# An attention stage whose softmax scaling moves behind the output product, in a lane of its own

## The chip, the cores and the metric

The kernel runs on one core of a Trainium2 chip. Five engines work from queues of their own: the matrix engine (PE in the profile, its weight loads shown apart as PEld), VectorE (DVE), ScalarE (ACT), GpSimd (POOL) and SyncE (SP), which here only issues transfers. SBUF is the working memory, PSUM the eight banks into which PE writes, DRAM the large memory outside. The metric is device time in microseconds (us) from the first to the last instruction of the program; smaller is better.

## The reference

Two layers over 1024 tokens of width 1024. Layer 0 mixes with a recurrence, layer 1 with attention; each layer then has a squared-ReLU MLP and a gated embedding. The change lies in the attention of layer 1, and in what stands around it:

```python
def chunk_band_attention(h, w_qkv, q_g, k_g, rel_bias):
    qkv = (h @ w_qkv).reshape(bsz, seq, 3, C_HEADS, C_HEAD_DIM)      # 16 heads x 64
    q = rmsnorm(qkv[:, :, 0], q_g) * (C_HEAD_DIM ** -0.5)
    k = rmsnorm(qkv[:, :, 1], k_g)
    v = qkv[:, :, 2]
    ...
        s = jnp.einsum('bqhd,bkhd->bhqk', q_c, k_b).astype(jnp.float32) + bias
        s = jnp.where(valid, s, -jnp.inf)
        prob = jax.nn.softmax(s, -1).astype(v.dtype)
        return jnp.einsum('bhqk,bkhd->bqhd', prob, v_b)              # own chunk of 64 and 8 before it
```

`h` is the RMS-normalised residual stream: each token's row is divided by the root of its mean square and multiplied by a learned gain. The result of the attention goes through `attn_w_out` and is added to the stream.

## The kernel before, in words

**Products.** Every value that enters a matmul is split into two parts (hi and lo, type float32r), and a product is three matmuls (hi with hi, hi with lo, lo with hi). ACT copies the hi part, DVE subtracts to get lo.

**Steps.** The attention runs over 16 steps `s = (pr, hf)`: `pr` is one of 8 pairs of heads, `hf` one of the two halves of the tokens (512 each). A step has three parts.

- `attn_in` projects: for each of 4 tiles of 128 tokens (`e`, tile number `i`) 24 matmuls of 128x384 give q, k and v of the pair in one PSUM bank. The gain is in `xg` already; the division by the root mean square is done after the product, as ACT copies q and k (`qk`) and v (`vs`) out of the bank with the factor `rscol[:, i]`. DVE subtracts for v's lo part. `rscol` is made once, in `row_stats`, right after the first projection: 16 small matmuls against ones sum POOL's squares (`accs`) over the width, and a chain of small DVE instructions takes the inverse root. Then POOL squares q and k, and DVE applies the head norm. At `hf == 0` the pair's weights (`load_qkv`, three loads of 512 KB) and bias tables (`toep`, two loads, three buffers) are loaded on SP's queue.
- `attn_norm` transposes q and k on PE into a dense bank, and ACT and DVE split them.
- `attn_block` is called for each of 2 heads `h` and 2 blocks `blk` of 256 queries. For each 128 queries `m` PE makes the scores against near keys (`sn`, bias added on DVE with a running maximum) and far keys (`sf`); ACT takes the exponential into `pb` and the sum over the row into `l`; DVE takes the reciprocal of the sum and ACT scales `pb` by it (L1973, L1974). After a pause `pb` is transposed on PE (`pt`), split (`ptile`, L349 and L350), and multiplied with v into `po`. At the second block the head's output is added up into `y` (128 rows: two heads of 64; 512 tokens), and after the second head `y` is stored to DRAM (`yd`, L2022).

**Who runs when.** `run` executes lanes (generators) in a simulated time: each lane traces instructions up to its next `yield`, and that yields a pause from the table `LAT` (in us), or a mark to wait for, such as `("at", s)`: step `s` finished. Of the lanes that are due, the first in the list goes on. There are two lanes of `attn_lane`, which share the blocks, then `attn_norms`, then `attn_ins`, which is at most three steps ahead of the finished ones. This order of tracing is the priority with which the compiler then orders each engine's queue; instructions of one engine run in that order.

**After the last step of projections** the lane `attn_ins` goes on with the gated embedding's projection (`ple_proj`) and the first half of the output projection (`out_early`), which reads `yd` back; four keys (marks) say what each of its parts waits for.

**PSUM.** Two banks (`dense`) serve projections and the transposes of the norms; in the attention two are for `sn`, one for `sf`, two for `pt`, one for `po`.

Of the kernel before, what the change touches and what calls it, by code (L numbers as in the profile page):

```python
# [8 lines left out]
F32 = mybir.dt.float32  # L9
# [8 lines left out]
P = 128  # L18
# [65 lines left out]
    "gdn_back4": 1.83,  # L84
    "attn_norm0": 0.24,
    "attn_block0": 0.97,
    "attn_block1": 4.45,
    "attn_block2": 0.43,
    "attn_block3": 0.94,
    "qk": 11.25,  # L90
    "norm": 1.28,
    "end_front": 46.33,
# [17 lines left out]
class Trunk:  # L110
# [252 lines left out]
            nc.scalar.activation(sq, src, AF.Square)  # L363
            nc.gpsimd.tensor_tensor(acc, acc, sq, op=ALU.add)

    def row_stats(self, accs, out, scale=1.0 / D, eps=1e-6):

        nc = self.nc
        nt = out.shape[-1]
        ps = self.stat_bank()  # L370
        for i in range(nt):
            self.mm(ps[:, i:i + 1], accs[i // 4][:, (i % 4) * P:(i % 4 + 1) * P], self.ones[:, 0:1],
                             start=True, stop=True)
        ms = self.sm.tile([P, NT], F32, tag="ms", name="ms")[:, 0:nt]
        nc.vector.tensor_scalar(ms, ps[:, 0:nt], scale, eps, op0=ALU.mult, op1=ALU.add)
        self.rsqrt_small(out, ms, [P, nt], "n")
# [1361 lines left out]
    def layer1_in(self):  # L1738
        nc, tc, a = self.nc, self.tc, self.a
        with ExitStack() as es:  # L1740
            self.psm = es.enter_context(self.pool("psml1", space=PSUM))
            wp = self.wp = es.enter_context(self.pool("l1a", 2))
            self.wr = es.enter_context(self.pool("l1wr", 2))
            self.w1 = es.enter_context(self.pool("l1w1"))
            l1 = es.enter_context(self.pool("l1", 2))
            self.sm = es.enter_context(self.pool("sml1", 2))
            self.yd = [[self.dr.tile([P, HB], F32, tag=f"yd{k}{hf}", name="yd") for hf in range(2)] for k in range(NK)]
            rbl = l1.tile([P, 16], F32, tag="rbl", name="rbl", bufs=1)
            nc.sync.dma_start(out=rbl, in_=a["rb_last"].rearrange("(o c) -> o c", o=1).broadcast_to((P, 16)))

            steps = [(pr, hf) for pr in range(8) for hf in range(2)]
            self.st = {}

            self.ql = [[pool.tile([P, HB], F32R, tag=tag, name="Ql", bufs=1) for pool, tag in
                        ((self.accp, f"acc{e}"), (l1, f"Ql{e}"))] for e in range(2)]
            jobs = iter([(s, h, b) for s in range(16) for h in range(2) for b in range(2)])
            self.run([self.attn_lane(steps, jobs, l1, rbl) for _ in range(2)] + [self.attn_norms(steps, l1), self.attn_ins(steps, l1)])

    def attn_ins(self, steps, l1):
        kv = {}  # L1760
        for s, (pr, hf) in enumerate(steps):
            if s >= 3:
                yield ("at", s - 3)
            self.st[s] = yield from self.attn_in(pr, hf, l1, kv)
            self.mark(("qk", s), self.lat["qk"])

        act = self.act
        ws = {}

        def load_w(src):  # L1770
            n = ws["n"] = ws.get("n", -1) + 1
            if n % 3 == 0:
                ws["h"], ws["l"] = self.weights3(n // 3 % 2)
            raw = self.wr.tile([P, T], F32, tag="wraw", name="wraw")
            self.nc.sync.dma_start(out=raw, in_=src)
            hi, lo = ws["h"][:, n % 3, :], ws["l"][:, n % 3, :]
            self.nc.scalar.copy(hi, raw)
            self.nc.vector.tensor_tensor(lo, raw, hi.bitcast(F32), op=ALU.subtract)
            return hi, lo
        p = [act([P, 2, T], F32R, "b") for _ in range(2)]  # L1780
        acc = act([P, 2, HB], F32)
        t = [act([P, 2, 2, HB], F32) for _ in range(4)]
        yield from self.ple_proj(1, lambda k, hf: p[k][:, :, hf * HB:hf * HB + HB], acc, lambda n: t[n // 2][:, n % 2],
                                 lambda: self.wp.tile([P, HB], F32, tag="sq", name="sq", bufs=1), load_w)
        q = {}

        def xt():
            n = q["n"] = q.get("n", -1) + 1
            if n % 4 == 0:
                q["x"] = act([P, 4, HB], F32)  # L1790
            return q["x"][:, n % 4, :]
        yield from self.out_early(1, self.xd, lambda q: act([P, 2, 2, HB], F32R), xt, load_w,
                                  [("at", 14), ("at", 14), ("at", 14), ("at", 15)])

    def attn_norms(self, steps, l1):
        K = []
# [10 lines left out]
    def attn_lane(self, steps, jobs, l1, rbl):  # L1807

        for s, h, b in jobs:
            yield ("in", s)  # L1810
            yield from self.attn_block(s, *steps[s], h, b, l1, rbl)

    def weights3(self, odd):

# [13 lines left out]
    def attn_in(self, pr, hf, l1, kv):  # L1828
# [15 lines left out]
        qk = wp.tile([P, 4, 256], F32, tag="qk", name="qk")  # L1844
        vs = l1.tile([P, 4, 2, P], F32R, tag="vs", name="vs", bufs=4)
        kv["vs"] = kv["vs"] + [vs]
        for e in range(4):
            i = 4 * hf + e
            ps = self.bank([P, 3, P])
            ts = slice(i * P, i * P + P)  # L1850
            for k in range(NK):
                ks = slice(k * P, k * P + P)
                xh, xl = self.xg[k][:, 0, ts], self.xg[k][:, 1, ts]
                self.mm(ps, xh, wh[:, :, ks], start=k == 0, stop=False)
                self.mm(ps, xh, wl[:, :, ks], start=False, stop=False)
                self.mm(ps, xl, wh[:, :, ks], start=False, stop=k == NK - 1)
                yield 0
            if pr == 0 and i == 0:
                self.row_stats(self.accs, self.rscol)
            rc = self.rscol[:, i:i + 1]  # L1860
            A.activation(qk[:, e, :], ps[:, 0:2, :].rearrange("p a c -> p (a c)"), AF.Copy, scale=rc)
            v3 = ps[:, 2, :].rearrange("p (h d) -> p h d", h=2)
            vf = vs[:, e].rearrange("p h c -> p (h c)").rearrange("p (q d) -> p q d", d=64)
            hi = vf[:, 0:4:3, :]
            A.activation(hi, v3, AF.Copy, scale=rc)
            V.scalar_tensor_tensor(vf[:, 1:3, :], v3, rc, hi.bitcast(F32), op0=ALU.mult, op1=ALU.subtract)  # L1866
            yield 0
        q4 = qk.rearrange("p i c -> p (i c)").rearrange("p (n d) -> p n d", d=64)
        ss = self.sm.tile([P, 16], F32, tag="ss1", name="ss1")
# [37 lines left out]
    def attn_block(self, s, pr, hf, h, blk, l1, rbl):  # L1907
# [36 lines left out]
        for j, (b, o, c0, c1) in place.items():  # L1944
            used[b] = max(used[b], o + c1 - c0)
        probs = []
        for m in (m0, m0 + 1):
            n0 = max(0, m - 2)
            nn = m - n0 + 1
            f0 = max(0, m - 4)  # L1950
            nf = n0 - f0
            pn = psm.tile([P, HB], F32, tag="sn", name="sn", bufs=2)
            score(pn[:, 0:nn * P], m, n0, nn)
            mx = sm.tile([P, 4], F32, tag="mx", name="mx", bufs=4)
            pb = self.wp.tile([P, 5 * P], F32, tag="pb", name="pb", bufs=4)
            S = pb[:, nf * P:(nf + nn) * P]
            V.tensor_tensor_reduce(S, pn[:, 0:nn * P], toep[:, (3 - nn) * P:], op0=ALU.add, op1=ALU.max,  # L1957
                                   scale=1.0, scalar=NEG, accum_out=mx[:, 0:1])
            l = sm.tile([P, 4], F32, tag="l", name="l", bufs=4)
            if nf:  # L1960
                pf = psm.tile([P, HB], F32, tag="sf", name="sf")
                score(pf[:, 0:nf * P], m, f0, nf)
                if m >= 4:
                    V.memset(pf[64:128, 0:64], NEG)
                V.reduce_max(mx[:, 1:2], pf[:, 0:nf * P], axis=AX.X)
                V.tensor_scalar(mx[:, 2:3], mx[:, 0:1], mx[:, 1:2], -1.0, op0=ALU.max, op1=ALU.mult)
                A.activation(pb[:, 0:nf * P], pf[:, 0:nf * P], AF.Exp, bias=mx[:, 2:3], accum_out=l[:, 1:2])
            else:
                V.tensor_scalar(mx[:, 2:3], mx[:, 0:1], -1.0, None, op0=ALU.mult)
            A.activation(S, S, AF.Exp, bias=mx[:, 2:3], accum_out=l[:, 0:1])  # L1970
            if nf:
                V.tensor_tensor(l[:, 0:1], l[:, 0:1], l[:, 1:2], op=ALU.add)
            V.reciprocal(l[:, 2:3], l[:, 0:1])  # L1973
            A.activation(pb[:, 0:(nf + nn) * P], pb[:, 0:(nf + nn) * P], AF.Copy, scale=l[:, 2:3])  # L1974
            probs.append((pb, f0))
            yield "attn_block0"
        yield "attn_block1"
# [30 lines left out]
                q += 1  # L2008
        if blk == 1:
            if h == 0:  # L2010
                st["y"] = l1.tile([P, HB], F32, tag="y", name="y", bufs=1)
            y, po = st["y"], st["po", h]
            oth = slice(64 * (1 - h), 64 * (1 - h) + 64)
            tmp = l1.tile([P, HB], F32, tag="otmp", name="otmp", bufs=1)
# [2 lines left out]
            if h == 1:  # L2017
                if s == 15:
                    yield ("ylast", 0)
                    self.split_scaled(self.ylast, y, None, slice(0, HB))  # L2020
                else:
                    nc.sync.dma_start(out=self.yd[pr][hf], in_=y)  # L2022
                self.dump("y1", y, (pr, slice(None), slice(hf * HB, hf * HB + HB)))
                self.mark(("at", s))
# [92 lines left out]
```

## Time and profile before

| | us |
|---|---|
| median of 3 runs | 3092.8 |
| lowest and highest | 3088.66, 3096.78 |
| the profiled execution | 3089.73 |
| its span, first to last instruction | 3088.0 |

The profiled execution's granted clock of PE is 0.978 of full speed on average. In time from the start of the span, layer 0 takes the first part, the projections of the attention begin at 1681, the first scores come at 1734, step 13 is finished at 2232 and step 15 at 2310; the rest is the output projection, the MLP and the gated embedding of layer 1.

A line of the profile such as `dps<-wq,act` names what an instruction writes and reads. `[4.11 <-POOL acc L1627]` says that the engine was idle for 4.11 us before it and that POOL's instruction of line 1627 ended that. Busy time of PE is modelled from pipelined matmuls; a stretch in which PE is busy throughout is not one in which it does its most.

### The profile page before, as it was taken

The page shows a single profiled execution, that of the slowest core. Times are in us where ns is not written, and L with a number is a line of the kernel's source. Part 1 is how long each engine was busy: PE and PEld are TensorE (multiplying, and loading weights), DVE is VectorE, ACT ScalarE, POOL GpSimd, SP SyncE. Part 2 cuts the span into 40 slices and gives each one's busy share as a digit, 9 for nine tenths or more (in the row PEclk, how much of TensorE's full clock was granted, in tenths as well). Part 3 has the DMA queues.
Part 4 walks back from the last instruction along what each step waited for, and adds up shares of the span by engine and source line. Part 5 has one row for each costly group of instructions (what it writes and reads, how often), then busy time and mean ns, then how long its engine had stood idle before and what let it go on. Part 6 is the DMA issues. An engine that isn't in the chain of part 4 may idle for free.

```text
span 3088.0 us, 47130 instructions
## 1 busy us (share of the span) xinstructions
PE 2979.5 (96%) x17288; PEld 2461.2 (80%) x17288; DVE 2232.1 (72%) x4518; ACT 1510.7 (49%) x2922; POOL 544.9 (18%) x978
## 2 busy tenths in 40 slices
PE   7999999999999999999999999989899999999999
PEld 5777778777777888888887988888788888888887
DVE  6656676657849788878867666766768888888762
ACT  4333443334427544444434577777756544544431
POOL 6533442443500000000015111100110000000002
PEclk9999999999999999999999999999999999999999
DMA  4211112211346434754424101100256444754432
GB/s 138 72 54 62 55 55 74 62 53 64 125 158 219 158 148 150 259 167 150 137 89 144 34 33 36 53 33 16 72 177 225 151 154 150 255 172 150 126 109 102
DMA packets 187639, 358.45 MB, mean 116 GB/s; under 512 B 45712, under 2 KB 47888, under 8 KB 187408
## 3 DMA queue, kind: packets, MB, share of 16 engines
q1 hardware_dynamic: 158608, 303.00, 29.6%
q10 hardware_dynamic: 28800, 52.44, 4.4%
q8 instruction: 136, 2.23, 0.3%
q14 instruction: 95, 0.78, 0.1%
HBM read 262.04 MB, written 93.32 MB: 115 GB/s over the span
## 4 chain that ended last, share of the span: by engine, by line
PE 79%; DVE 10%; ACT 4%; DMA 3%; POOL 2%; issue 2%; SPq 0%; DVEq 0%; POOLq 0%; ACTq 0%
PE dps L177 66%; PE ch L177 2%; PE pm L177 2%; PE iz L177 1%; PE po L177 1%; PE tp L177 1%; DVE ptile L350 1%; PE pt L192 1%; DVE pb L1957 1%; PE sn L177 1%; POOL subt L415 1%; PE py L177 1%; DMA wraw<-in_w_qkv 1%; ACT pb L1970 1%; POOL sub L417 1%
## 5 line engine op out<-in xcount | busy, mean ns | idle before, releaser
L177 PE MATMUL dps<-r,act 128*128 128x512 f32 x3528 | 829.4, 392 | 0.0
L177 PEld LDWEIGHTS dps<-r,act 128*128 128x128 f32 x3528 | 662.0, 188 | 145.8
L177 PE MATMUL dps<-xg,whi 128*128 128x512 f32 x1280 | 434.0, 419 | 14.9 <-ACT xg L352 7.4
L1614 POOL TENSOR_TENSOR pn<-pn,prs 128x512 f32<-128x512 f32 x32 | 47.1, 1474 | 1543.1 <-ACT prs L386 1447.7
L177 PE MATMUL dps<-wq,act 128*128 128x384 f32 x1536 | 305.7, 345 | 6.4 <-DVE vs L1866 3.1
L177 PEld LDWEIGHTS dps<-xg,whi 128*128 128x128 f32 x1280 | 233.9, 195 | 67.9 <-issue 8.0
L177 PEld LDWEIGHTS dps<-wq,act 128*128 128x128 f32 x1536 | 266.6, 191 | 10.5 <-DVE vs L1866 4.9
L177 PE MATMUL dps<-xg,wlo 128*128 128x512 f32 x640 | 258.8, 405 | 1.3 <-DVE wlo L304 1.3
L177 PE MATMUL dps<-late,act 128*128 128x512 f32 x960 | 229.2, 392 | 0.0
L177 PEld LDWEIGHTS dps<-late,act 128*128 128x128 f32 x960 | 180.3, 188 | 39.7
L1271 ACT CAST act<-act 128x512 fp32r<-128x512 f32 (+1 forms) x223 | 137.6, 649 | 131.6 <-PE dps L177 67.5
L1384 DVE TENSOR_TENSOR late<-late,dps 128x512 f32<-128x512 f32 x224 | 152.4, 684 | 52.2 <-PE dps L177 45.8
L1271 ACT CAST act<-late 128x512 fp32r<-128x512 f32 x210 | 124.2, 617 | 133.2 <-PE dps L177 90.4
L177 PE MATMUL dps<-act 128*128 128x512 f32 x672 | 165.0, 392 | 0.0
L1272 DVE TENSOR_TENSOR act<-act 128x512 fp32r<-128x512 f32 (+1 forms) x223 | 154.8, 721 | 6.0 <-ACT act L1271 5.8
L177 PEld LDWEIGHTS dps<-act 128*128 128x128 f32 x672 | 126.1, 188 | 28.7
L1272 DVE TENSOR_TENSOR act<-late,act 128x512 fp32r<-128x512 f32 x210 | 141.5, 688 | 8.9 <-ACT act L1271 7.0
L177 PEld LDWEIGHTS dps<-xg,wlo 128*128 128x128 f32 x640 | 124.4, 194 | 29.2 <-DVE wlo L304 1.8
L303 ACT CAST whi<-wraw 128x1024 fp32r<-128x1024 f32 x78 | 81.9, 1050 | 122.0 <-PE dps L177 82.4
L1522 DVE TENSOR_TENSOR xw<-xw,dps 128x512 f32<-128x512 f32 x174 | 118.0, 683 | 31.5 <-PE dps L177 31.5
L177 PE MATMUL dps<-xw,act 128*128 128x512 f32 x576 | 139.6, 392 | 0.0
L1389 ACT ACTIVATE late<-late 128x512 f32<-128x512 f32 x128 | 80.3, 630 | 119.4 <-DVE late L1384 113.5
(484 smaller groups left out, 5656.7 us busy)
## 6 DMA issues: line engine op xcount, KB each, us to landing
hb<-late ACTq DMA_DIRECT2D x168, 256.0 KB
act<-hb SPq DMA_DIRECT2D x138, 256.0 KB
late<-in_w SPq DMA_DIRECT2D x60, 512.0 KB
wraw<-in_w_in SPq DMA_DIRECT2D x56, 512.0 KB
act<-in_w SPq DMA_DIRECT2D x96, 256.0 KB
braw<-hb SPq DMA_DIRECT2D x72, 256.0 KB
wraw<-in_w_out SPq DMA_DIRECT2D x21, 512.0 KB
wraw<-in_w_qkv SPq DMA_DIRECT2D x21, 512.0 KB
```

The lines of the kernel that those rows point to most:

```text
L177: return self.begin(self.nc.tensor.matmul(out, lhsT, rhs, start=start, stop=stop, skip_group_check=again))
L192: return self.begin(self.nc.tensor.transpose(out, in_, ident))
L303: nc.scalar.copy(hi, raw)
L350: nc.vector.tensor_tensor(dst[:, 1, sl], src, dst[:, 0, sl].bitcast(F32), op=ALU.subtract)
L415: E.tensor_tensor(o, X[:, 0:i, i:i + 1].broadcast_to((NP, i, n)), Bq[:, i:i + 1, i + 1:16].broadcast_to((NP, i, n)), op=ALU.mult)
L417: E.tensor_tensor(X[:, 0:i, i + 1:16], X[:, 0:i, i + 1:16], o, op=ALU.add)
L1271: A.copy(hi, s)
L1272: V.tensor_tensor(lo, s, hi.bitcast(F32), op=ALU.subtract)
L1384: V.tensor_tensor(r, t, u, op=ALU.add)
L1389: A.activation(t, t, AF.Relu)
L1522: V.tensor_tensor(x[n][:, hs[hf]], x[n][:, hs[hf]], ps, op=ALU.add)
L1614: G.tensor_tensor(pn, pn, prs[:, sl], op=ALU.mult)
```

## The change

Two things are changed.

First, the division by the softmax sums. For steps 0 to 13 ACT no longer scales `pb`; unscaled exponentials go through the transposes and the product with v. The reciprocals of the sums go into a small tile per step (`rl`, 128 queries x 2 heads x 4 tiles). A new lane, `attn_sums`, third in the list, waits for each of these steps to be finished, stores `rl` to DRAM so that a head's 512 numbers lie in a row (each element of 4 bytes goes to a place of its own), pauses 14.00, loads each head's row back into 64 partitions (`R`), pauses 4.00, multiplies `y` by `R` on DVE and stores it. Steps 14 and 15 scale `pb` as before. `y` has two buffers instead of one. The pause before the transposes is 3.70 instead of 4.45, and the first two keys of `out_early` name the new lane's end.

Second, the opening of the stage. The first two projections use the `sn` banks, the third a dense one, and `row_stats` comes after the third, in a `pt` bank; the copies out of the three banks are held until then. All later projections are copied out as before.

```diff
-    "attn_block1": 4.45,
+    "attn_block1": 3.70,
+    "attn_sums0": 14.00,
+    "attn_sums1": 4.00,
...
-            self.run([self.attn_lane(steps, jobs, l1, rbl) for _ in range(2)] + [self.attn_norms(steps, l1), self.attn_ins(steps, l1)])
+            self.run([self.attn_lane(steps, jobs, l1, rbl) for _ in range(2)] + [self.attn_sums(steps, l1)] + [self.attn_norms(steps, l1), self.attn_ins(steps, l1)])
...
-                                  [("at", 14), ("at", 14), ("at", 14), ("at", 15)])
+                                  [("sums", 14), ("sums", 14), ("at", 14), ("at", 15)])
...
+    def attn_sums(self, steps, l1):
+        nc = self.nc
+        for s, (pr, hf) in enumerate(steps[:14]):
+            yield ("at", s)
+            rd = self.dr.tile([1, T], F32, tag="rd", name="rd", bufs=2)
+            nc.sync.dma_start(out=rd.rearrange("o (m q) -> (o q) m", m=8), in_=self.st[s]["rl"].rearrange("p h m -> p (h m)"))
+            yield "attn_sums0"
+            R, y = l1.tile([P, HB], F32, tag="R", name="R", bufs=1), self.st[s]["y"]
+            for h in range(2):
+                nc.sync.dma_start(out=R[64 * h:64 * h + 64], in_=rd[:, h * HB:h * HB + HB].broadcast_to((64, HB)))
+            yield "attn_sums1"
+            nc.vector.tensor_tensor(y, y, R, op=ALU.mult)
+            nc.sync.dma_start(out=self.yd[pr][hf], in_=y)
+        yield ("at", 14)
+        self.mark(("sums", 14))
...
+            if pr == 0 and i < 2:
+                ps = psm.tile([P, HB], F32, tag="sn", name="dps", bufs=2)[:, 0:3 * P].rearrange("p (a c) -> p a c", a=3)
+            else:
+                ps = self.bank([P, 3, P])
...
-            if pr == 0 and i == 0:
-                self.row_stats(self.accs, self.rscol)
-            rc = self.rscol[:, i:i + 1]
...
+            held.append((i, e, ps))
+            if pr == 0 and i == 2:
+                self.row_stats(self.accs, self.rscol, bank=psm.tile([P, HB], F32, tag="pt", name="st", bufs=2))
+            if pr or i > 1:
+                for h in held:
+                    scale(*h)
+                held.clear()
...
+        if h == 0 and blk == 0:
+            st["rl"] = sm.tile([P, 2, 4], F32, tag="rl", name="rl", bufs=4)
...
-            V.reciprocal(l[:, 2:3], l[:, 0:1])
-            A.activation(pb[:, 0:(nf + nn) * P], pb[:, 0:(nf + nn) * P], AF.Copy, scale=l[:, 2:3])
+            rl = st["rl"][:, h, m % 4:m % 4 + 1]
+            V.reciprocal(rl, l[:, 0:1])
+            if s > 13:
+                A.activation(pb[:, 0:(nf + nn) * P], pb[:, 0:(nf + nn) * P], AF.Copy, scale=rl)
...
-                st["y"] = l1.tile([P, HB], F32, tag="y", name="y", bufs=1)
+                st["y"] = l1.tile([P, HB], F32, tag="y", name="y", bufs=2)
...
-                else:
+                elif s == 14:
                     nc.sync.dma_start(out=self.yd[pr][hf], in_=y)
```

More of the change, by code (lines that the diff above doesn't have):

```diff
@@ L364, in sumsq, with row_stats @@
             nc.gpsimd.tensor_tensor(acc, acc, sq, op=ALU.add)
-    def row_stats(self, accs, out, scale=1.0 / D, eps=1e-6):
+    def row_stats(self, accs, out, scale=1.0 / D, eps=1e-6, bank=None):
         nc = self.nc
         nt = out.shape[-1]
-        ps = self.stat_bank()
+        ps = bank if bank is not None else self.stat_bank()
         for i in range(nt):
@@ L1846, in attn_in, with scale @@
         kv["vs"] = kv["vs"] + [vs]
+        def scale(i, e, ps):
+            rc = self.rscol[:, i:i + 1]
+            A.activation(qk[:, e, :], ps[:, 0:2, :].rearrange("p a c -> p (a c)"), AF.Copy, scale=rc)
+            v3 = ps[:, 2, :].rearrange("p (h d) -> p h d", h=2)
+            vf = vs[:, e].rearrange("p h c -> p (h c)").rearrange("p (q d) -> p q d", d=64)
+            hi = vf[:, 0:4:3, :]
+            A.activation(hi, v3, AF.Copy, scale=rc)
+            V.scalar_tensor_tensor(vf[:, 1:3, :], v3, rc, hi.bitcast(F32), op0=ALU.mult, op1=ALU.subtract)
+        held = []
         for e in range(4):
             i = 4 * hf + e
-            ps = self.bank([P, 3, P])
+            if pr == 0 and i < 2:
+                ps = psm.tile([P, HB], F32, tag="sn", name="dps", bufs=2)[:, 0:3 * P].rearrange("p (a c) -> p a c", a=3)
+            else:
+                ps = self.bank([P, 3, P])
             ts = slice(i * P, i * P + P)
@@ L1857, in attn_in @@
                 yield 0
-            if pr == 0 and i == 0:
-                self.row_stats(self.accs, self.rscol)
-            rc = self.rscol[:, i:i + 1]
[L1861 to L1866, printed above, removed]
+            held.append((i, e, ps))
[5 more added lines that the diff above has]
+                held.clear()
             yield 0
```

## The prediction

> **What bounds the kernel now.** I read the page first (shares of the engines), then busy time by stretches, to find where the matrix engine idles, then who makes it wait there, and last the timeline at the two places that the change touches. The first fence is the page, the second the stretches around the attention stage (its columns are the stretch, its length, then busy time and instructions of PE, PEld, DVE, ACT and POOL, the granted clock, the DMA share and GB/s).
>
> ```profile
> span 3088.0 us, 47130 instructions
> PE 2979.5 (96%) x17288; PEld 2461.2 (80%) x17288; DVE 2232.1 (72%) x4518; ACT 1510.7 (49%) x2922; POOL 544.9 (18%) x978
> ```
>
> ```profile
> 1690.00:1700.00 10.00, 7.26 (x25) 7.18 (x26) 6.18 (x15) 3.77 (x5) 5.59 (x8) 0.52 0.51 180
> 1700.00:1710.00 10.00, 10.00 (x58) 10.00 (x57) 1.39 (x3) 1.47 (x4) 1.04 (x1) 0.97 0.14 52
> ...
> 1684.00:1740.00 56.00, 48.28 (x260) 46.21 (x258) 28.78 (x79) 21.88 (x45) 15.13 (x17) 0.91 0.26 87
> 1740.00:2232.00 492.00, 449.91 (x2852) 420.81 (x2851) 350.48 (x1148) 365.82 (x867) 57.37 (x60) 0.98 0.12 39
> 2232.00:2310.00 78.00, 74.25 (x389) 63.45 (x388) 53.66 (x134) 49.80 (x103) 12.55 (x9) 0.93 0.51 174
> 2310.00:3088.00 778.00, 772.87 (x3384) 632.39 (x3382) 586.70 (x909) 348.85 (x577) 21.71 (x16) 1.00 0.47 159
> ```
>
> PE is the bound. After the attention it idles 5.1 us in 778, so an earlier end of the attention ends the kernel earlier by as much. In the 492 us of steps 0 to 13 PE idles 42.1 us; at the stage's opening it idles 7.7 of 56 us, and ten of those run at a granted clock of 0.52. These two idle times are what the change can win. In the 492 us ACT is busy 74% and DVE 71%, but unevenly:
>
> ```profile
> 1838.00:1842.00 4.00, 3.15 (x24) 2.52 (x23) 3.47 (x9) 3.99 (x11) 1.04 (x1) 1.00 0.00 0
> 1870.00:1874.00 4.00, 2.02 (x14) 1.48 (x13) 1.43 (x8) 3.90 (x13) 0.00 (x0) 1.00 0.00 0
> 1874.00:1878.00 4.00, 3.53 (x16) 3.33 (x17) 3.19 (x11) 1.89 (x8) 0.00 (x0) 0.58 0.00 0
> 1886.00:1890.00 4.00, 2.28 (x10) 1.96 (x10) 3.90 (x13) 3.30 (x10) 0.00 (x0) 0.79 0.00 0
> 1910.00:1914.00 4.00, 2.09 (x18) 1.78 (x17) 2.97 (x9) 4.00 (x11) 1.04 (x1) 1.00 0.01 2
> ```
>
> Where PE idles, ACT is full (3.90 to 4.00 of 4 us) in three of these, DVE (3.90) in one. Whom PE waits for in steps 0 to 13 (waiter, awaited, us in total, times, longest):
>
> ```profile
> PE pt L192 <- ACT pb L1974: 8.4, 9, 1.8
> PE po L177 <- ACT ptile L349: 6.6, 14, 1.0
> PE po L177 <- DVE ptile L350: 6.1, 11, 1.4
> PE sf L177 <- ACT pb L1967: 4.0, 7, 1.5
> PE pt L192 <- DVE ptile L350: 4.0, 9, 0.9
> PE dps L192 <- DVE vs L1866: 3.1, 6, 1.0
> ```
>
> **Term 1: three projections ahead of the statistics.** The timeline at the opening:
>
> ```profile
> 1685.81 0.45 PE L177 MATMUL dps<-wq,act 128*128 128x384 f32 x1 [0.32 <-DVE act L353]
> 1686.93 1.05 PE L177 MATMUL dps<-ones,acc 128*128 128x1 f32 x8 [0.68 <-POOL acc L1627]
> 1692.09 1.86 PE L177 MATMUL dps<-ones,acc 128*128 128x1 f32 x8 [4.11 <-POOL acc L1627]
> 1694.60 27.96 PE L177 MATMUL dps<-wq,act 128*128 128x384 f32 x144 [0.64 <-DVE ms L375]
> 1696.59 0.17 DVE L291 SCALAR_TENSOR_TENSOR rscol<-rsw,rscol 128x8 f32<-128x8 f32 x1
> 1697.55 0.47 ACT L1861 ACTIVATE qk<-dps,rscol 128x256 f32<-128x256 f32 x1
> 1697.92 0.36 ACT L1865 ACTIVATE vs<-dps,rscol 128x128 fp32r<-128x128 f32 x1
> 1698.82 0.34 DVE L1866 SCALAR_TENSOR_TENSOR vs<-dps,rscol,vs 128x128 fp32r<-128x128 f32 x1
> 1710.11 0.47 ACT L1861 ACTIVATE qk<-dps,rscol 128x256 f32<-128x256 f32 x1 [3.42 <-PE dps L177]
> 1714.27 0.47 ACT L1861 ACTIVATE qk<-dps,rscol 128x256 f32<-128x256 f32 x1 [3.42 <-PE dps L177]
> ```
>
> The first projection ends at 1686.26. The statistics then wait 0.68 and 4.11 us for POOL's sum of squares, and the next projection 0.64 us for their bank. Projections 1 and 2 need only the first half of the tokens, which is there. At full clock one takes 4.16 us (1714.27 less 1710.11). Changed: projections 1 and 2 end at 1694.6; the sum (there at 1692.09) is no longer waited for; 16 statistic matmuls at the undisturbed price of 1.05 per 8 end at 1696.7; projection 3 ends at 1700.9. Before, projection 4 was done at 1714.2. New is that three results are held until the statistics' inverse root, which took 2.8 us from the last statistic matmul (1693.95 to 1696.76): 1699.5. Then each pair of ACT scalings takes 0.73 us and the DVE part ends 1.24 after the last ACT start; the third held result frees its bank at about 1702.6. Projection 4 has only the two dense banks, waits 1.7 us and ends at 1706.8. Gain 1714.2 - 1706.8 = **7.4 us**. Bounds: 9.1 without the new wait; 2.4 if that wait halves the clock as in the 0.52 row (ten us at half cost five). Scores need the two lent sn banks only after a whole step's projections and norms, so lending them costs nothing; were they needed at once, it would be the 2.2 us of the three held scalings.
>
> On that wait: 2.0 us of idle in 1870 to 1874, in pieces, was followed by a clock of 0.58, so a total of idle, not one long wait, can do it here. [...]
>
> **Term 2: the scaling on ACT goes for steps 0 to 13.** The first two rows are the L1974 instructions alone by stretch (ACT busy after the length), the others one block's chain:
>
> ```profile
> 1733.00:2232.00 499.00, 76.69 (x115) 0.98 0.12 40
> 2232.00:2310.00 78.00, 9.48 (x13) 0.93 0.51 174
> ```
>
> ```profile
> 1846.16 0.60 ACT L1970 ACTIVATE pb<-pb,mx 128x384 f32<-128x384 f32 x1
> 1847.08 0.17 DVE L1973 RECIPROCAL l<-l 128x1 f32<-128x1 f32 x1
> 1847.34 0.83 ACT L1974 ACTIVATE pb<-pb,l 128x640 f32<-128x640 f32 x1 [0.49 <-DVE l L1973]
> ```
>
> 112 of 128 scalings go, about 75 of 86.2 us; ACT falls from 74% to 59% of the stretch. The reciprocals stay (written elsewhere, same shape, no cost). The transposes can start at the exponential's end (1846.76) instead of the scaling's (1848.17), 1.41 us earlier. The planner's pause before them falls by 0.75 (4.45 to 3.70), so it issues them earlier too and only 0.66 us per block is slack. Nine waits on the scaling lose 0.66 each: 5.9 of 8.4; I take 5.5. ACT's other waits (6.6 + 4.0) shrink as its load falls by a fifth and its queue more than that; I take 4. Those ended by DVE (6.1 + 4.0 + 3.1) stay: DVE's split of the transposed block is what is late next. **9.5 us** together. Bounds: 0, if DVE's work ends all these waits instead, and 19.0, all waits ended by ACT.
>
> **Term 3: the lane of sums.** Per step it issues one store of 128x8 sums in pieces of 4 bytes, two loads of 256 KB together, one DVE product of 128x512 and the y store, which only moves. DVE gains 14 instructions:
>
> ```profile
> L1384 DVE TENSOR_TENSOR late<-late,dps 128x512 f32<-128x512 f32 x224 | 152.4, 684 | 52.2 <-PE dps L177 45.8 <-issue 3.1 <-ACT late L1472 1.4
> ```
>
> 14 x 0.684 = 9.6 us. Bounds 0 and 9.6; DVE idles 29% of the time and its quoted waits are a third of PE's idle, so I take **2 us** lost. SP issues 42 more transfers; its rows (last: longest wait), and a weight load from issue to landing on the chain of waits:
>
> ```profile
> SPq L1841 <- DVE mx L1957: 268.6, 13, 23.0
> SPq L422 <- DMA z<-sub: 22.6, 15, 3.5
> SPq L400 <- DMA scr<-N: 15.6, 6, 4.1
> 1859.00 3.73 DMA wraw<-in_w_qkv
> ```
>
> SP idles most of the stage (268.6 us in the bias loads' waits), which covers the 42 issues; without it they would cost what stands behind them: bias and weight loads. The loads of R wait on SP for the store; behind them stand those loads and y stores, whose readers are POOL, ACT and later steps. The product waits on DVE for R; behind it are the splits, and PE waits for those. Stores to DRAM that SP had to await took 1.5 (22.6/15) to 4.1 us, a load of 512 KB 3.73. So the trip takes 5 to 8 us against 18 planned (14.00 + 4.00). A store in 4-byte pieces is in no row; I take 8 us, no wait. The second y buffer keeps the late y store off the next step. The change of key for the output projection names steps that are done by then, cost nothing; without that cover, the trip of step 13.
>
> [...]
>
> **The sum.** 7.4 + 9.5 - 2 = 14.9 us off the profiled execution's 3089.73: 3074.8. The median of the runs is 3.1 us higher, 3092.8; from it, 3078. About 0.3% (9.3 us) is what a measurement of this kernel can tell from no change.
>
> **The rivals.**
> - A, slower: the product waits for R. R's load stands behind a bias load on SP that waits up to 23.0 us, more than the 18 planned; then DVE, and PE with it, stands still. It decides from (7.4 + 9.5 - 2)/14 = 1.1 us per step; at 2.5 us per step 35 us: 3092.8 - 15 + 35 = 3113. For it: the 268.6 us. Against: the store is awaited 4.1 us at most in the rows, so R's load can go out soon after a step's end; how often a bias load stands ahead of it then, the rows don't say.
> - B, ACT's relief is hidden: DVE's splits end the same waits, term 2 is 0, 3092.8 - 7.4 + 2 = 3087. For it: 13.2 us of waits on DVE already. Against: ACT full in three of the four idle stretches.
> - C, the opening only moves its wait to projection 4 and the clock halves: term 1 is 2.4, 3092.8 - 9.9 = 3083.
> - D, more: all ACT-ended waits go, the DVE waits that follow ACT shrink by half (6.6), and the dips of the clock to 0.58 and 0.79 with them (some 3 us): 7.4 + 19 + 6.6 + 3 = 36, 3057.
>
> **Chances.** Forecast 0.52, B 0.16, C 0.10, D 0.10, A 0.12. The forecast's own range is 3067 to 3087 (the ends of terms 1 and 2 do not fall together). Faster by over 0.3% (below 3083.5): most of the forecast (0.46), half of C, D: 0.61. Same: the rest of the forecast, half of C, B: 0.27. Slower: A, 0.12. The range 3056 to 3094 leaves out A and the far end of D, 0.16 in all.
>
> **What would show it.** Term 1: the statistics' matmuls after three projections, no wait on POOL, no 0.52 row, and a wait under 2 us before projection 4. Term 2: ACT near 59% in steps 0 to 13, no PE wait on a scaling, PE idle near 35 instead of 42 us. Term 3: no DVE wait on R. The prediction is wrong if DVE waits for R, if waits on DVE's split grow to the 19 us that ACT gave back, or if the clock dips more often.

## The result and the profile after

The changed kernel took 3131.1 us (median of 4, 3128.9 to 3134.0); the kernel before, beside it, 3093.9 (median of 4). The ratio is 1.0123, with a 95% interval of 1.0105 to 1.0140: 37 us slower, where 15 us less was forecast. Sign and range are both wrong. The profiled execution took 3133.95 us.

The page of the changed kernel, from its first part and from the chain of work that ended last:

```profile
span 3131.9 us, 47160 instructions
PE 2993.3 (96%) x17288; PEld 2473.9 (79%) x17288; DVE 2233.4 (71%) x4532; ACT 1441.6 (46%) x2810; POOL 545.1 (17%) x978
...
PE 74%; DVE 11%; DMA 8%; ACT 3%; POOL 2%; issue 2%; SPq 0%; DVEq 0%; POOLq 0%; ACTq 0%
PE dps L179 63%; DMA rd<-rl 3%; PE ch L179 2%; PE pm L179 1%; PE iz L179 1%; DMA R<-rd 1%; PE tp L179 1%; PE po L179 1%; DMA act<-in_w 1%; DMA wraw<-in_w_qkv 1%; PE py L179 1%; PE pt L194 1%; DVE ptile L352 1%; DVE pb L1988 1%; POOL sub L419 1%
```

ACT's busy time falls by 69 us, as it should, and the span grows all the same. The store of the sums (`rd<-rl`) and the load of them (`R<-rd`) now stand in the chain, with 3% and 1% of the span.

Its busy time by stretches (columns as in the prediction):

```profile
1710.00:1716.00 6.00, 1.38 (x9) 1.06 (x7) 4.11 (x16) 2.56 (x9) 1.04 (x1) 0.91 0.36 115
1716.00:1722.00 6.00, 6.00 (x20) 6.00 (x21) 3.06 (x12) 0.15 (x1) 1.04 (x1) 0.52 0.00 1
...
1740.00:2232.00 492.00, 433.61 (x2738) 412.45 (x2737) 335.70 (x1106) 276.81 (x709) 54.57 (x53) 0.96 0.14 39
2232.00:2310.00 78.00, 65.02 (x346) 54.64 (x346) 62.35 (x179) 55.95 (x131) 19.69 (x15) 0.87 0.43 145
2310.00:3132.00 822.00, 814.86 (x3591) 667.32 (x3590) 610.58 (x954) 368.62 (x612) 21.69 (x16) 1.00 0.47 159
```

In the 492 us from 1740 PE is busy 433.61 instead of 449.91, at a granted clock of 0.96 instead of 0.98, and gets through 2738 matmuls instead of 2852. The rest spills into the next stretch. ACT is at 56%. So it is not that another engine became full: DVE is busy less than before too (335.70, before 350.48).

Whom the engines wait for between 1680 and 2360, four rows of the list (waiter, awaited, us in total, times, longest):

```profile
DVE y L1827 <- DMA R<-rd: 56.3, 14, 6.8
PE po L179 <- DVE ptile L352: 29.9, 18, 5.5
SPq L1825 <- DMA rd<-rl: 139.2, 14, 10.6
SPq L1860 <- DVE mx L1988: 138.8, 12, 22.7
```

The product `y * R` (L1827) keeps DVE standing in each of the 14 steps, from 0.3 to 6.8 us and 4.0 on average; the prediction's rival A put the break-even at 1.1. PE's waits for DVE's split of the transposed block grow from 6.1 to 29.9 us. And SP waits 139.2/14 = 9.9 us for each store of the sums.

One trip, that of step 0, in three views: the chain of work, then DVE's timeline, then SP's (start, length, instruction, and in brackets the idle time before it).

```profile
1760.49 10.93 DMA rd<-rl
1771.96 3.37 DMA R<-rd
```

```profile
1760.30 0.16 DVE L2005 RECIPROCAL rl<-l 128x1 f32<-128x1 f32 x1
...
1770.95 0.69 DVE L2049 TENSOR_TENSOR y<-po,otmp 64x512 f32<-64x512 f32 x1
1771.67 0.56 DVE L1988 CUSTOM_DVE_ANT_0 pb<-sn,toep 128x384 f32<-128x384 f32 x1
1772.16 0.08 DVE L1988 DVE_READ_ACCUMULATOR2_ANT mx<- 128x1 f32 x1
1772.16 0.17 DVE L291 TENSOR_TENSOR rsw<-nn 128x16 f32<-128x16 f32 x1
1775.45 0.69 DVE L1827 TENSOR_TENSOR y<-y,R 128x512 f32<-128x512 f32 x1 [3.12 <-DMA R<-rd]
```

```profile
1760.49 0.38 SPq L1821 DMA_DIRECT2D rd<-rl  x1
1771.44 1.11 SPq L1825 DMA_DIRECT2D R<-rd  x2
1772.64 0.54 SPq L1860 DMA_DIRECT2D toep<-in_rb  x1
```

The step's last reciprocal is there at 1760.46 and the store goes out at once, some 10 us before the step's last sum into `y`. It is seen complete 10.93 us later, and R's load goes out at that moment, ahead of the bias load (`toep`), not behind it. The load takes 3.4 us more. The product, however, stands in DVE's queue only three short instructions behind that last sum, which is done at 1771.64. In this step DVE reaches the product 11.8 us after the store goes out and can start it 15.0 us after: a wait of 3.12 us. Over the 14 steps DVE is there after 10.6 us on average (7.3 to 15.0) and the product starts after 14.6 (14.1 to 16.0); the difference is the 4.0 us. The 18 us of pauses in the planner are nowhere to be seen.

The opening, on PE and DVE:

```profile
1691.05 3.83 PE L179 MATMUL dps<-wq,act 128*128 128x384 f32 x21
1696.26 9.13 PE L179 MATMUL dps<-wq,act 128*128 128x384 f32 x51 [1.38 <-ACT act L354]
1705.23 1.84 PE L179 MATMUL st<-ones,acc 128*128 128x1 f32 x16
1706.93 4.41 PE L179 MATMUL dps<-wq,act 128*128 128x384 f32 x24
1715.97 15.38 PE L179 MATMUL dps<-wq,act 128*128 128x384 f32 x72 [4.62 <-DVE vs L1873]
```

```profile
1710.15 1.23 DVE L1844 TENSOR_TENSOR wq<-wraw,wq 128x1024 fp32r<-128x1024 f32 x1 [3.35 <-ACT wq L1843]
1711.29 0.16 DVE L377 TENSOR_SCALAR ms<-st 128x8 f32<-128x8 f32 x1
```

The wait on POOL's sums is gone, as forecast. But the statistics, complete at 1707.07, are first read at 1711.29: in DVE's queue a split of the next weights stands ahead and waits 3.35 us. PE then waits 4.62 us before the fifth projection (projection 4 in the prediction's count, which starts at 0) instead of the 1.7 forecast, and the clock is at 0.52 right after (the stretch from 1716).

### The profile page after: what moved, and what is told of

Same layout as the page of the kernel before. It is cut to its first block, busy times and chain, and to the rows that moved or that the text cites. A ratio compares the mean times of both kernels' runs of the same rounds, so it can differ in the third digit from the quotient of the medians.

```text
span 3131.9 us, 47160 instructions
## 1 busy us (share of the span) xinstructions
PE 2993.3 (96%) x17288; PEld 2473.9 (79%) x17288; DVE 2233.4 (71%) x4532; ACT 1441.6 (46%) x2810; POOL 545.1 (17%) x978
## 4 chain that ended last, share of the span: by engine, by line
PE 74%; DVE 11%; DMA 8%; ACT 3%; POOL 2%; issue 2%; SPq 0%; DVEq 0%; POOLq 0%; ACTq 0%
PE dps L179 63%; DMA rd<-rl 3%; PE ch L179 2%; PE pm L179 1%; PE iz L179 1%; DMA R<-rd 1%; PE tp L179 1%; PE po L179 1%; DMA act<-in_w 1%; DMA wraw<-in_w_qkv 1%; PE py L179 1%; PE pt L194 1%; DVE ptile L352 1%; DVE pb L1988 1%; POOL sub L419 1%
## 5 line engine op out<-in xcount | busy, mean ns | idle before, releaser
L179 PEld LDWEIGHTS dps<-wq,act 128*128 128x128 f32 x1536 | 271.3, 194 | 18.4 <-DVE vs L1873 10.1
L179 PE MATMUL po<-ptile,vs 128*128 128x256 f32 (+1 forms) x576 | 107.6, 298 | 35.3 <-DVE ptile L352 29.9
```

The lines of the kernel that those rows point to most:

```text
L179: return self.begin(self.nc.tensor.matmul(out, lhsT, rhs, start=start, stop=stop, skip_group_check=again))
```

## The experiments

The theory to test: the loss is DVE's standing still for R, since the store in 4-byte pieces is slow and the product is early in DVE's queue. Its rivals: the instructions' new order alone costs the time; the stores' many small packets disturb other transfers; or it is the opening. Three groups were measured, each on a chip of its own and beside the kernel before: the first four beside 3094.2 us (median of 22), the next four beside 3092.6 (of 11), the last two beside 3092.3 (of 11). A ratio is that to the kernel before, with its 95% interval in brackets; kernels of different groups are best compared by it.

**The opening alone.** The scaling on ACT is back and the lane is out (so are, in lines not shown, the second y buffer and the changed keys):

```diff
-    "attn_block1": 3.70,
+    "attn_block1": 4.45,
...
-            self.run([self.attn_lane(steps, jobs, l1, rbl) for _ in range(2)] + [self.attn_sums(steps, l1)] + [self.attn_norms(steps, l1), self.attn_ins(steps, l1)])
+            self.run([self.attn_lane(steps, jobs, l1, rbl) for _ in range(2)] + [self.attn_norms(steps, l1), self.attn_ins(steps, l1)])
...
-            if s > 13:
+            if True:
...
```

> The kernel before with the opening alone: three projections ahead of the statistics, the scaling on ACT kept, no lane of sums, the pause at 4.45. Theory W (the loss is DVE standing still for R): no loss here; the opening ends the fourth projection some 4 us earlier than before, so 3090, between 3086 and 3094. Rival P (the opening, with its 4.6 us wait and the half clock behind it, costs): 3100 or more.

Measured: 3087.4 us, ratio 0.9976 [0.9960, 0.9992]. The opening is a gain of 6.8 us (2.5 to 12.4) and not the cause of the loss.

**The lane alone.** The opening is as in the kernel before (its banks too):

```diff
...
-            if pr == 0 and i == 2:
-                self.row_stats(self.accs, self.rscol, bank=psm.tile([P, HB], F32, tag="pt", name="st", bufs=2))
-            if pr or i > 1:
-                for h in held:
-                    scale(*h)
-                held.clear()
+            if pr == 0 and i == 0:
+                self.row_stats(self.accs, self.rscol)
+            for h in held:
+                scale(*h)
+            held.clear()
```

> The changed kernel with the opening undone: statistics after the first projection, as before. Theory W: 14 waits of DVE on R of some 4 us each stay, the time is that of the changed kernel and up to 4 us more, 3131 to 3136. Rival P: it falls to 3095 to 3110.

Measured: 3119.7 us, ratio 1.0072 [1.0044, 1.0101]. The loss is there without the opening: it comes with the lane. DVE's wait in this kernel:

```profile
DVE y L1827 <- DMA R<-rd: 49.4, 13, 7.0
```

The expected 3131 and more was missed: this kernel is 11 us faster than the whole change, though it lacks the opening's gain. Of the 11.0 us between the two profiled spans, 5.3 lie ahead of the first projection (it starts at 1691.0 with the whole change, 1685.7 here) and 6.5 behind the last sum of y, in stages that the edit doesn't touch. The waits for R are 6.9 us shorter in all. Why the medians differ by as much stays open.

**No division.** The lane is left out and the scaling stays away, so that steps 0 to 13 are not divided by their sums:

```diff
-            self.run([self.attn_lane(steps, jobs, l1, rbl) for _ in range(2)] + [self.attn_sums(steps, l1)] + [self.attn_norms(steps, l1), self.attn_ins(steps, l1)])
+            self.run([self.attn_lane(steps, jobs, l1, rbl) for _ in range(2)] + [self.attn_norms(steps, l1), self.attn_ins(steps, l1)])
...
```

> The changed kernel without the lane of sums: ACT's scaling gone for steps 0 to 13, no store of the sums, no R, no product, y stored at once (leaves out the division by the softmax sums in these steps). Opening, pause of 3.70 and two y buffers kept. Theory W: the 56 us of DVE's waits are gone and ACT's relief shows, 3076 to 3086. Rival O (the new order of instructions and more stretches at half clock cost, whatever DVE waits for): 3110 or more.

Measured: 3078.6 us, ratio 0.9944 [0.9928, 0.9961]. Without it PE is busy 457.55 us in a stretch of 492 us of the stage, where the changed kernel had 433.61:

```profile
1733.00:2225.00 492.00, 457.55 (x2945) 433.65 (x2944) 364.86 (x1200) 307.49 (x785) 66.52 (x61) 0.98 0.13 41
```

So taking the scaling off ACT is a gain by itself, and the lane adds some 52 us on top.

**A later product.** The same trip, but the product of a step is tied, in DVE's queue, behind the first head's sum of the next step:

```diff
-            yield "attn_sums1"
-            nc.vector.tensor_tensor(y, y, R, op=ALU.mult)
+            yield ("pv", 4 * s + 5)
+            mul = nc.vector.tensor_tensor(y, y, R, op=ALU.mult)
+            self.tc.add_manual_dep(mul.ins, self.yadd[s + 1].ins.name, mybir.DependencyInfo(
+                mybir.DependencyClass.NoSync, mybir.DependencyReason.DATA), reason="order")
```

> The changed kernel with each product y*R tied behind the first head's sum of the next step in DVE's queue (12 to 25 us after the step's end instead of at once), nothing taken out: same stores, loads and products. Theory W: R has landed by then, DVE's waits on R fall from 56 us to under 15, and the time to 3078 to 3092. Rival O: no change, 3120 or more. Rival S (the 4-byte stores disturb other transfers): 3110 or more with DVE's waits on R gone.

Measured: 3084.8 us, ratio 0.9968 [0.9956, 0.9980]. Its waits of DVE and SP:

```profile
DVE y L1827 <- DMA R<-rd: 10.6, 3, 4.0
SPq L1825 <- DMA rd<-rl: 103.6, 13, 10.9
```

The store is still awaited 8.0 us on average and 10.9 at the longest. What is gone is most of DVE's standing still, 56.3 to 10.6 us, and with it all the loss against the kernel before; 6.2 us above the kernel without division remain. This speaks for the wait; but the order of the queues changed too, so two kernels with the order of the change kept follow.

**A constant R.** Store and loads are out, the product multiplies by ones. In the two traces PE, DVE and ACT issue the same instructions in the same order from the first to the last:

```diff
-            rd = self.dr.tile([1, T], F32, tag="rd", name="rd", bufs=2)
-            nc.sync.dma_start(out=rd.rearrange("o (m q) -> (o q) m", m=8), in_=self.st[s]["rl"].rearrange("p h m -> p (h m)"))
...
-            R, y = l1.tile([P, HB], F32, tag="R", name="R", bufs=1), self.st[s]["y"]
-            for h in range(2):
-                nc.sync.dma_start(out=R[64 * h:64 * h + 64], in_=rd[:, h * HB:h * HB + HB].broadcast_to((64, HB)))
+            if s == 0:
+                R = l1.tile([P, HB], F32, tag="R", name="R", bufs=1)
+                nc.gpsimd.memset(R, 1.0)
+            y = self.st[s]["y"]
```

> The changed kernel with no store of the sums and no loads: the product multiplies y by a tile of ones that stays in SBUF (leaves out the division in steps 0 to 13). The queues of DVE and PE hold the same instructions in the same order as the changed kernel. Theory W: with nothing to wait for, the 37 us over the kernel before and more are gone: 3079 to 3087; the 14 products cost 0 to 8 us against the run without any division (3078.6). Rival O: the order alone costs, 3110 or more.

Measured: 3078.9 us, ratio 0.9952 [0.9933, 0.9972]. With the same order and no trip the loss is gone: the order is not the cause. The 14 products are still there, by the groups view (busy us and mean ns, idle before):

```profile
L1826 DVE TENSOR_TENSOR y<-y,R 128x512 f32<-128x512 f32 x14 | 10.1, 722 | 0.1
```

Against the kernel without any division they cost 0.3 us by the medians and 2.5 by the ratios (0.9952 against 0.9944), which can't be told from nothing, nor from the 2 us forecast.

**A contiguous store.** One word is changed: each partition's 8 sums go to 32 adjacent bytes, 128 pieces instead of 1024 (the sums come back in the wrong order). The traces again show the order of PE, DVE and ACT of the changed kernel:

```diff
-            nc.sync.dma_start(out=rd.rearrange("o (m q) -> (o q) m", m=8), in_=self.st[s]["rl"].rearrange("p h m -> p (h m)"))
+            nc.sync.dma_start(out=rd.rearrange("o (q m) -> (o q) m", m=8), in_=self.st[s]["rl"].rearrange("p h m -> p (h m)"))
```

> The changed kernel with the sums stored as they lie, 128 pieces of 32 bytes instead of 1024 of 4 bytes, all else the same (the sums come back in the wrong order, so the division uses wrong sums). DVE's and PE's queues are unchanged. Theory W with cause 'pieces': the store is awaited 1.5 to 3 us on SP instead of 9.9, R comes 7 to 8 us earlier, DVE's waits on R vanish or fall under 10 us, 3080 to 3092. Rival 'fixed trip' (any store and load through DRAM takes as long as this one): SP still waits 8 us or more, 3125 to 3135.

Measured: 3077.6 us, ratio 0.9946 [0.9927, 0.9966]. Its wait of SP, then step 0 on SP and on DVE:

```profile
SPq L1825 <- DMA rd<-rl: 18.5, 14, 2.6
```

```profile
1760.95 0.33 SPq L1821 DMA_DIRECT2D rd<-rl  x1
1763.29 1.11 SPq L1825 DMA_DIRECT2D R<-rd  x2
```

```profile
1771.42 0.69 DVE L2049 TENSOR_TENSOR y<-po,otmp 64x512 f32<-64x512 f32 x1
...
1772.72 0.68 DVE L1827 TENSOR_TENSOR y<-y,R 128x512 f32<-128x512 f32 x1
```

The store is awaited 1.3 us instead of 9.9; R's load goes out 2.3 us after the store, not 10.95; the product stands at the same place in all 14 steps, and nothing is waited for. The number of bytes, transfers and instructions is the same, so the cutting into pieces alone (their size, and with it their number) makes the 50 us. The time is 2.4 us below the range expected; the rival's range begins 47 us above it. The run doesn't show whether small packets disturb other transfers a little; it shows that there is no loss left for them to explain.

**A transposed store.** The whole computation, with the sums turned on DVE first (blocks of 32x32), so that four stores write pieces of 128 bytes in the right order:

```diff
-            nc.sync.dma_start(out=rd.rearrange("o (m q) -> (o q) m", m=8), in_=self.st[s]["rl"].rearrange("p h m -> p (h m)"))
+            rt = self.sm.tile([P, 32], F32, tag="rt", name="rt", bufs=2)
+            nc.vector.transpose(rt, self.st[s]["rw"])
+            for g in range(4):
+                nc.sync.dma_start(out=rd.rearrange("o (m g q) -> g (o m) q", m=8, g=4)[g], in_=rt[32 * g:32 * g + 8])
...
-            st["rl"] = sm.tile([P, 2, 4], F32, tag="rl", name="rl", bufs=4)
+            st["rw"] = sm.tile([P, 32], F32, tag="rl", name="rl", bufs=4)
+            G.memset(st["rw"][:, 8:32], 0.0)
+            st["rl"] = st["rw"][:, 0:8].rearrange("p (h m) -> p h m", h=2)
```

> The full computation: DVE transposes the 128x8 sums in blocks of 32 and four stores of 8 pieces of 128 bytes take them to DRAM; product placed by the compiler as in the changed kernel. Theory W with cause 'pieces': each step costs one small DVE transpose and three more SP issues, but SP waits 2 to 3 us instead of 9.9 and DVE's waits on R fall under 15 us: 3080 to 3095. Rival 'fixed trip': 3120 or more.

Measured: 3074.5 us, ratio 0.9933 [0.9915, 0.9951]; it is faster than the kernel before and the changed one, and 5.5 us below the range expected. In its profile, the 14 turns on DVE by the groups view, SP's wait, and the stage's stretch:

```profile
L1822 DVE STREAM_TRANSPOSE rt<-rl 128x32 f32<-128x32 f32 x14 | 2.9, 209 | 0.3
```

```profile
SPq L1828 <- DMA rd<-rt: 12.6, 20, 1.8
```

```profile
1740.00:2232.00 492.00, 457.55 (x2955) 432.62 (x2955) 375.67 (x1226) 309.96 (x791) 71.62 (x76) 0.99 0.15 49
```

For 2.9 us of DVE (and a small POOL instruction and three more issues on SP in each step) the store's landing leaves the path: DVE waits for R no more. PE is as busy as with no division at all, so the lane is hidden.

**The transposed store with the later product.** Both of these edits together, in part:

```diff
+            nc.vector.transpose(rt, self.st[s]["rw"])
...
-            yield "attn_sums1"
-            nc.vector.tensor_tensor(y, y, R, op=ALU.mult)
+            yield ("pv", 4 * s + 5)
+            mul = nc.vector.tensor_tensor(y, y, R, op=ALU.mult)
...
```

> The transposed store and the product tied behind the first head's sum of the next step. Theory W: no DVE wait on R at all, and the 10.6 us in three waits that the late product alone kept are gone: 3077 to 3084, ahead of both kernels. Rival O: no better than the late product alone (3084.8).

Measured: 3075.5 us, ratio 0.9935 [0.9914, 0.9956]: no gain over the transposed store, and faster than the late product alone. With a short trip the product's place no longer matters; it was the two together.

**The transposed store without the opening.** The edit of "the lane alone" on top of the transposed store:

```diff
-            if pr == 0 and i == 2:
-                self.row_stats(self.accs, self.rscol, bank=psm.tile([P, HB], F32, tag="pt", name="st", bufs=2))
+            if pr == 0 and i == 0:
+                self.row_stats(self.accs, self.rscol)
...
```

> The transposed store with the opening undone: statistics after the first projection. It tells what the opening is worth once DVE does not wait for R. If the opening alone (3087.4 against 3094.2) adds up with the lane: 4 to 8 us above the transposed store, 3078 to 3083. If the opening disturbs the lane's steps, as the lane alone (3119.7) against the changed kernel (3131.1) could mean: 3065 to 3074.

Measured: 3071.4 us, ratio 0.9940 [0.9925, 0.9956]. The expected rise of 4 us or more did not show. The time lies in the range of the other case, but does not prove it: by the medians this kernel is 3 us faster than the transposed store, by the ratios (0.9940 against 0.9933) 2 us slower, and neither can be told from nothing. What the opening is worth beside a lane that works stays open.

**The statistics' root first.** On the transposed store: the three weight splits of the second pair are tied, on DVE, behind the inverse root of the statistics.

```diff
-            nc.vector.tensor_tensor(wl[:, j, :], raw, wh[:, j, :].bitcast(F32), op=ALU.subtract)
+            lo = nc.vector.tensor_tensor(wl[:, j, :], raw, wh[:, j, :].bitcast(F32), op=ALU.subtract)
+            if pr == 1:
+                self.tc.add_manual_dep(lo.ins, self.root.ins.name, mybir.DependencyInfo(
+                    mybir.DependencyClass.NoSync, mybir.DependencyReason.DATA), reason="order")
```

> The transposed store, and on DVE the three splits of the second pair's weights tied behind the statistics' inverse root. If the 4.6 us wait of PE before the fifth projection came from the statistics' first DVE instruction standing in the queue behind a split that waits for its weights: the wait falls to under 2 us and the time by 2 to 5 us, 3069 to 3073. If it came from the three held scalings, as the prediction had it: the wait stays above 4 us and the time at 3074.5.

Measured: 3070.7 us, ratio 0.9930 [0.9917, 0.9943]. PE's timeline, then the stretch behind the wait:

```profile
1687.47 3.83 PE L179 MATMUL dps<-wq,act 128*128 128x384 f32 x21
...
1708.52 12.77 PE L179 MATMUL dps<-wq,act 128*128 128x384 f32 x72 [1.41 <-DVE vs L1880]
```

```profile
1710.00:1722.00 12.00, 11.73 (x70) 11.46 (x68) 6.18 (x17) 3.19 (x8) 1.53 (x2) 1.00 0.23 77
```

The wait is 1.41 us and the clock stays at 1.00. The first seven projections take 33.8 us (1687.47 to 1721.29). In the changed kernel it was 40.3, from 1691.05 to 1731.35. In the kernel before it was 41.8: its seventh ended at 1722.56 (the prediction's row from 1694.60), and its first began here:

```profile
1680.72 3.83 PE L177 MATMUL dps<-wq,act 128*128 128x384 f32 x21
```

So the opening is 8.0 us shorter than before the change, but the time of the whole, 3070.7 against 3074.5 for the transposed store, has overlapping intervals and doesn't prove the gain. Against the transposed store without the opening, of the same group, it is 0.7 us, within the noise too.

## Why the prediction was wrong

**Term 3 is the step that failed**: "the trip takes 5 to 8 us against 18 planned", "I take 8 us, no wait". Both numbers fell. The trip takes 14.6 us, since a store in 4-byte pieces is awaited 9.9 us and not the 1.5 to 4.1 of the rows for stores in larger pieces. I wrote that no row has such a store, and took its time from those that the trace had; the bound for an unseen kind of transfer was too tight. And the 18 us don't exist on the chip. They are the planner's, which orders the program's text. The product's place in DVE's queue is fixed with the program: it is the first to the eighth instruction behind the step's last sum, the same in each step whether R is late (the changed kernel) or early (the contiguous store). DVE got there 10.6 us after the store went out, on average, and 14.6 less 10.6 is the 4.0 us per step that it stands still. Taking away either fault takes away the loss: the piece size (contiguous, transposed) or the place (later product).

With the same sums in pieces of 32 and of 128 bytes the stores were awaited 1.3 and 0.9 us per step (18.5/14 and 12.6/14).

**Rival A** had the effect, its break-even (1.1 us per step; it came to 4.0) and the path from DVE to PE right. Its place was wrong: R's load doesn't stand behind a bias load, it goes out as soon as the store is seen complete, in all 14 steps 9.5 to 11.0 us after the store. Its price of 35 us came from an assumed 2.5 us per step; at the measured 4.0, 14 steps make 56 us, and the kernel lost 52 against the one without division.

**The 2 us for the products** fit: with the trip away they cost 0.3 to 2.5 us, which can't be told from nothing. DVE, busy 71% of the changed kernel's span, has the room, as argued.

**Term 2, 9.5 us**, holds. ACT is at 63% in the transposed store's stretch (309.96/492) where 59% was forecast; much of the rest is later work that now falls into the same 492 us (nine scalings of steps 14 and 15 alone are 5.1 us). PE idles 34.5 us there, as forecast (near 35, before 42.1). By the waits of PE between 1740 and 2232, the part ended by ACT's work on the blocks (8.4 + 6.6 + 4.0 before) is 10.5 us with the transposed store (rows of the list):

```profile
PE pt L194 <- DVE ptile L352: 6.9, 13, 0.9
PE po L179 <- DVE ptile L352: 5.2, 11, 1.1
PE dps L179 <- DVE F L1934: 4.3, 6, 1.0
PE po L179 <- ACT ptile L351: 4.1, 6, 0.8
PE pt L194 <- ACT pb L2003: 3.8, 4, 1.1
PE sf L179 <- ACT pb L2003: 1.8, 3, 0.9
PE pt L194 <- ACT pb L2006: 0.8, 3, 0.3
```

19.0 less 10.5 is 8.5 us; the rest of the waits ended by ACT, on other work, comes to 2.5 us before and 3.6 after. No wait on a scaling is left, and DVE's split of the transposed block is late next, as the step said; its waits grow only from 10.1 to 12.1, so rival B (the relief is hidden) is out. The times agree: the kernel without division, which has the shorter pause and the second y buffer too, is 8.8 us faster than the opening alone.

**Term 1, 7.4 us**, had the right mechanism and one instruction overlooked. The wait for POOL went, and the new one before projection 4 came, but as 4.6 us, since the split of the second pair's weights stands ahead of the statistics in DVE's queue. That is rival C: the clock halves (0.52 from 1716 to 1722), and the first seven projections are 1.5 us shorter in the changed kernel, where the step gave 7.4 and, with the clock halved, 2.4. With the split behind the statistics, the wait is 1.41 (forecast 1.7) and the opening 8.0 us shorter (7.4).

The 7.4 takes it that the forecast wait of 1.7 us leaves the clock whole. That was the author's estimate, and no run shows it. The prediction's row from 1870, with 2.0 us of idle and a clock of 0.58 behind it, speaks against it, since most of that idle was one wait and not pieces:

```profile
1872.90 0.88 PE L192 MATMUL pt<-ident,pb 128*128 128x128 f32 x6 [1.75 <-ACT pb L1974]
```

At projection 4 the clock was 1.00 behind the 1.41 us of idle (the statistics' root first) and 0.52 behind the 4.62 (the changed kernel). Two other waits of PE, both in the execution with the contiguous store, say more. Here they are, and the stretch behind each with its clock (0.50 and 1.00):

```profile
1699.51 10.70 PE L179 MATMUL dps<-wq,act 128*128 128x384 f32 x51 [1.80 <-ACT act L354]
1719.04 12.76 PE L179 MATMUL dps<-wq,act 128*128 128x384 f32 x72 [2.88 <-DVE vs L1873]
```

```profile
1702.00:1704.00 2.00, 2.00 (x8) 2.00 (x7) 1.21 (x2) 1.24 (x2) 1.32 (x2) 0.50 1.07 374
1720.00:1722.00 2.00, 2.00 (x14) 2.00 (x13) 1.07 (x4) 0.00 (x0) 0.80 (x1) 1.00 0.01 4
```

After the wait of 2.88 us the clock was 1.00; after the shorter one of 1.80 us it was 0.50. So the length of a single wait alone doesn't settle it in these traces. What does stays open, and with that whether the forecast wait of 1.7 us would always have left the clock whole.

In the time of the whole kernel, the opening alone gained 6.8 us (its first seven projections are 2.8 us shorter: 1685.13 to 1724.12), and beside the transposed store nothing that can be measured. Which of the two holds stays open: the time up to the first projection moved between 1679.7 and 1693.9 us from one profiled execution to another, more than the whole term, though PE, DVE and ACT issue the same instructions in the same order up to there in all twelve.

**The sum.** The forecast of 3078 is near where the change lands once its trip is quick: 3074.5 with the transposed store, 3077.6 with the contiguous one. In part that is luck, since the same time comes without the opening (3071.4), whose 7.4 us are in the sum. Term 2 stood, term 1 had its mechanism but no settled size, and term 3 was mis-sized by 50 us. A chance of 0.12 for it was too low for a store that no row priced, in front of an engine whose queue runs in order.

## What to carry to other kernels

Price a trip through DRAM by its pieces: a transfer that scatters single elements is not bounded by rows of larger pieces (9.9 us here, where the rows had 1.5 to 4.1), and turning the data on the chip first may cost almost nothing (0.21 us of DVE per step here, against some 9 us of landing). When an in-order engine gets an instruction that waits for a transfer, look up where it will stand in that engine's compiled queue, not where the plan of the program puts it. And compare the time from the store to that place (10.6 us on average here) with the trip (14.6).

## What the runs showed of the hardware

- 1024 pieces of 4 bytes were awaited 9.9 us, 128 pieces of 32 bytes 1.3 us, with the same 4 KB: the landing went with the pieces, not the bytes. How it splits within the DMA engines no view shows.
- More waiting on PE came with a lower clock: with DVE standing 4 us per step, PE idled 58.4 of the 492 us and the granted clock was 0.96; before the change it was 42.1 us and 0.98, with the transposed store 34.5 us and 0.99. The order is not strict: with the lane alone it was 53.3 us and 0.95.
- The clock did not go by the length of a single wait alone: after 1.80 us of idle it was 0.50, after 2.88 and after 1.41 us 1.00, after 4.62 us 0.52.
- 14 products of 0.69 us on an engine at 71% cost nothing that can be measured, while 14 waits of 4.0 us on the same engine cost 52 us: in a queue that runs in order, what stood behind the product stood still with it, and PE's waits for DVE's split rose from 6.1 to 29.9 us.
